# The first block of a SwiGLU feed-forward: x's parts in another order, and two of its eight pairs in groups of seven products

## The chip, the cores and the metric

The kernel runs on one core of a Trainium2 chip. The metric is the device time of one execution in microseconds. Three runs of the kernel before took 2275.22, 2275.67 and 2276.53 us; their median is 2275.67.

The engines are called as in the profile: PE (TensorE) does the matrix products, DVE (VectorE) and ACT (ScalarE) the elementwise work, SP issues nearly all the DMA transfers. Each engine takes its instructions in the order in which the program issued them.

## What is computed

The reference is one decoder layer on 256 tokens of width 2048, in float32. The change lies in the very first matrix product of it, `x @ w_gu`:

```python
def swiglu(x, w_gu, w_down):
    g, u = jnp.split(x @ w_gu, 2, axis=-1)
    return (jax.nn.silu(g) * u) @ w_down

h = layer_norm(alpha * h + 0.5 * swiglu(h, w_ffn1_gu[i], w_ffn1_down[i]), ln_g[i, 0], ln_b[i, 0])
# then: retention and attention branches, gated and mixed; layer_norm
h = layer_norm(alpha * h + 0.5 * swiglu(h, w_ffn2_gu[i], w_ffn2_down[i]), ln_g[i, 2], ln_b[i, 2])
# then: a gated embedding; layer_norm
```

`w_gu` is 2048 x 11264 and `w_down` 5632 x 2048.

## The kernel before

**Numbers in two parts.** Every operand of a product is held as a high part (a copy in the reduced type float32r, made by ACT, line 100) and a low part (value minus high part, made by DVE, line 101). A product of two values is three matrix instructions: low by high, high by high, high by low (lines 376, 377, 378, `Sum.add`). Each is 128 x 128 by 128 x 512.

**Blocks, pairs and units.** The gate and up stage of the first feed-forward ("f1") runs over 11 blocks. A block has 512 columns of the gate half and 512 of the up half, for 256 tokens (two halves of 128), so four outputs of 128 x 512, each in a bank of PSUM: `f1g` (two) and `f1u` (two). The 2048 rows of the weight are taken in eight pairs of 128-row steps, numbered 0 to 7. A plain pair (letter "P") is two units (`Single`): one 512 KB weight transfer for the gate columns, then one for the up columns, with 12 matrix instructions each.

**Seven products.** A pair with letter "S" (`Seven`) does the 2 x 2 by 2 x 2 product of its quarters in seven products in place of eight, so 21 matrix instructions for 24. It loads the same two transfers, makes four sums of quarters of the weight on DVE (lines 172 to 175), the high and low parts of seven of the quarters and sums, and needs four sums of quarters of x as well: the "forms" (`seven_forms`, lines 447 to 450, then a cast and a low part). Forms 0 serve pairs 0 and 1, forms 1 pairs 2 and 3. Four of the seven products go to sums of their own, p1, p6, p7 and q5, a PSUM bank each, shared by all S pairs of the block; the other three go to outputs. Behind the block's last S pair the `fold` (`seven_common`) copies p1 to SBUF on ACT (line 481), and combines it with p6 (482), p7 (483) and q5 (484, 485) on DVE; at the block's end the four outputs are added (line 964), and Silu and the gate product follow. A block without S pairs has neither: two Silu on ACT (line 970), two products on DVE (line 972). In f1, block 0 is "PPPPPPPP" with pairs 0 to 7 in order, odd blocks are "PPSPSPSP" (pairs 0, 1, 2 as S, and the others in order between them), even blocks "PPSSPSSP" (0 to 3 as S). In the last S pair of a block the products for the four own sums come first, p1, q5, p6, p7.

**PSUM.** The pool has eight banks. A bank is given to a tile at its first product and comes back when its last reader has been issued; it is taken in the order in which banks came back.

**x.** x comes in four parts of 128 x 4 x 256 (512 KB, `xraw`); part c serves pairs 2c and 2c + 1. `load_x_chunk` issues the transfer and the split into `xt`. Part 0 is loaded in three pieces with the first two weight units; part 1 directly behind; parts 2 and 3 at positions 2 and 4 of block 0 (`first_chunk`). The parts are kept for the forms, both of which are made at position 7 of block 0.

**The order of the work.** The program is written in one order, and a small planner puts loads and conversions into it. `fill` is called whenever a unit is `done`: it converts the next loaded unit as long as the converted ones stand for less than 45 units of time (12 for a plain unit, 21 for a grouped pair) and slots are left, and issues loads while converted and loaded ones stand for less than 90. Slots are SBUF tiles of 4 KB a partition; the planner is allowed 9 of them at first and 24 from position 6 of block 0. `block` calls `before(u)` ahead of position u: that is where x's parts, the constants (four small transfers issued by ACT, lines 806 to 809) and the forms come in. In a grouped pair, `done(u)`, and so `fill`, comes before `fold`.

```python
            for to, left, right in steps:
                to.add(left, right)
            done(u)
            run_side()
            if p == sevens[-1]:
                fold(p1.ap, p6.ap, p7.ap, q5.ap)
```

Of the kernel before, what the change touches and what calls it, by code (L numbers as in the profile page):

```python
# [38 lines left out]


SEVEN = (0, 1, 2, 3)


AHEAD = (4, 5)
# [13 lines left out]
def layer(ctx: ExitStack, tc: tile.TileContext, io):  # L58
# [13 lines left out]
    def banks(name):  # L72
        return [bank(name + str(j)) for j in range(2)]

    def slot(shape, dt, name):
        return slots.tile(shape, dt, tag="slot", name=name)
# [225 lines left out]
    def slots_for_weights(n, ahead=45, far=90):  # L302
        room.update(slots=n, ahead=ahead, far=far)
# [136 lines left out]
    def seven_forms(full, hi, lo):  # L440


        a11, a21 = (full[:, 0::2, t * P : (t + 1) * P] for t in range(2))
        a12, a22 = (full[:, 1::2, t * P : (t + 1) * P] for t in range(2))
        raw = slot([P, 8, P], F32, "sums")
        f5, f6, f7, f3 = (raw[:, 2 * j : 2 * j + 2, :] for j in range(4))
        dve.tensor_tensor(f5, a21, a22, ALU.subtract)
        dve.tensor_tensor(f7, a11, a21, ALU.subtract)
        dve.tensor_tensor(f6, f5, a11, ALU.subtract)
        dve.tensor_tensor(f3, a12, f6, ALU.add)  # L450
        split(hi, lo, raw)
        return lambda e: [(hi[:, 2 * j + e, :], lo[:, 2 * j + e, :]) for j in range(4)]
# [9 lines left out]
    def forms_of(parts, name):  # L462
        hi, lo = (slot([P, 8, P], F32R, name + w) for w in "hl")
        return seven_forms(whole(parts, name + "w"), hi, lo)

    def units_of(order, sevens, ahead=()):

        sevens, ahead = list(sevens), list(ahead)
        plain = [p for p in range(KD // 2) if p not in sevens + ahead]
        of = {"S": sevens, "D": ahead, "P": plain}  # L470
        return [(kind, of[kind].pop(0)) for kind in order]
# [6 lines left out]
    def seven_common(p1, p6, p7, q5):  # L478

        e, w = slot([P, 2, 512], F32, "eve"), slot([P, 2, 512], F32, "evw")  # L480
        act.copy(e[:, 0], p1)
        dve.tensor_tensor(w[:, 0], e[:, 0], p6, ALU.add)
        dve.tensor_tensor(e[:, 1], w[:, 0], p7, ALU.add)
        dve.tensor_tensor(w[:, 0], q5, w[:, 0], ALU.subtract)
        dve.tensor_tensor(w[:, 1], q5, e[:, 1], ALU.subtract)
        return e, w
# [6 lines left out]
    def plan_tokens(key, n_k, nk=2):  # L493
        for c in range(n_k // nk):
            plan.append(Single(key + (c,)))
# [309 lines left out]
    def load_constants():  # L805
        act.dma_start(cst, io["cst"])
        act.dma_start(mask, io["mask"])
        act.dma_start(gn, io["gn"])
        act.dma_start(sink, io["att_sinks"].broadcast_to([P, HA]))
# [42 lines left out]


    def gu_units(name, j):
        if j == 0:
            return [("P", p) for p in range(KD // 2)]
        if name == "f2" and j in AHEAD_BLOCKS:
            return units_of("PPSDSDSP", SEVEN[:3], AHEAD)
        order = "PPSSPSSP" if j % 2 == 0 else "PPSPSPSP"
        return units_of(order, SEVEN[: order.count("S")])  # L860

    def gu_keys(name, j):
        return lambda n, p: (name + "_gu", j, n, p)
# [26 lines left out]
    def ffn(name, i, ht, norm, keep, residual, keepers, away):  # L890
# [23 lines left out]
        def convert(g):  # L914
            hi, lo = (slot([P, 4, S], F32R, f"{name}a{w}{g}") for w in "hl")
            split(hi, lo, raws[g])
            acts[g] = hi, lo

        for j in range(KF // 4):
            pg, pu = banks(f"{name}g{j}"), banks(f"{name}u{j}")  # L920
            units = gu_units(name, j)
            n_of = {(0, 0): KD, (0, 1): KD, (1, 0): KD, (1, 1): KD}
            for kind, p in units:
                if kind != "P":
                    for at in ((0, 0), (0, 1), (1, 0)):
                        n_of[at] -= 1
                    n_of[1, 1] -= 2
            sums = [[Sum((pg, pu)[n][t], n_of[t, n]) for n in range(2)] for t in range(2)]
            got = []

            if norm is not None and j == 0:
                front, units = units[:FRONT_PAIRS], units[FRONT_PAIRS:]
                steps = [(gu_keys(name, 0)(n, p), 2 * p, n) for _, p in front for n in range(2)]
                norm.first(steps, rhs, sums, (
                    (3, (1, 0)), (5, "more"), (5, (1, 1)), (7, (0, 2)), (8, (1, 2)), (9, (0, 3)), (10, (1, 3)), (10, "go"),
                ))
                slots_for_weights(24)

            def before(u, j=j, offset=KD // 2 - len(units)):
                u += offset  # L940
                if j == 0 and norm is None and u % 2 == 0:
                    first_chunk(u // 2)
                    if u == 6:
                        slots_for_weights(24)
                    if u == 2:
                        load_constants()
                if j == 0 and u == 7:
                    for g in sorted({p // 2 for p in SEVEN}):
                        hi, lo = (slot([P, 8, P], F32R, f"{name}f{w}{g}") for w in "hl")
                        made[g] = seven_forms(keep[g], hi, lo)  # L950
                    if name == "f2":
                        g = AHEAD[0] // 2
                        made[g] = forms_of([ht[:, 4 * g : 4 * g + 4, :]], f"{name}f{g}")
                if name == "f2" and j in AHEAD_BLOCKS and u == 0:
                    slots_for_weights(AHEAD_SLOTS - j)
                if j == KF // 4 - 1 and u in (4, 6):
                    convert(u // 2 - 2)

            block(f"{name}{j}", units, gu_keys(name, j), rhs, forms, sums, lambda *a: got.extend(seven_common(*a)), before)
            if got:  # L960
                g, v = got
                for x, ps in ((g, pg), (v, pu)):
                    for t in range(2):
                        dve.tensor_tensor(x[:, t], x[:, t], ps[t], ALU.add)  # L964
                act.activation(g, g, AF.Silu)  # L965
                dve.tensor_tensor(v, g, v, ALU.mult)
            else:
                v = slot([P, 2, 512], F32, f"{name}v{j}")
                for t in range(2):
                    act.activation(v[:, t], pg[t], AF.Silu)  # L970
                for t in range(2):
                    dve.tensor_tensor(v[:, t], v[:, t], pu[t], ALU.mult)
            later(2, lambda j=j, v=v: turned(j, v))
# [71 lines left out]
        norm = Norm((2, 3), sums, combine, y, stats, i, 4 * LN_EPS, keepers, away, (0, 3))  # L1045
# [55 lines left out]
    def later(n, job):  # L1101
        for j in range(n):
            if len(side) <= j:
                side.append(idle)
        side.insert(n, job)
# [515 lines left out]
            held_out(steps, lhs, [[s] for s in sums], lambda t, j: None, first_done, lambda n: None, 0)  # L1621
            last_half()

    def first_chunk(c):

        if c == 0:
            load_x_chunk(0)
            fill()
        if c < 3:
            load_x_chunk(c + 1)  # L1630

    x_parts = {}

    def load_x_chunk(c):
        raw = slot([P, 4, S], F32, f"xraw{c}")
        x_parts[c] = raw
        if c:
            sync.dma_start(raw, io["xT"][c])
            split_x(c, slice(0, 4))
            return  # L1640
        parts = [slice(0, 1), slice(1, 2), slice(2, 4)]
        for at in parts:
            sync.dma_start(raw[:, at], io["xT"][c][:, at])
        for queue in (act, sync):
            u = plan.pop(0)
            u.load(pieces=2, queue=queue)
            u.chunk.make_hi()
            room["used"] += u.keeps
            ready.append(u)
        first, second = (u.chunk for u in ready)  # L1650
        split_x(c, parts[0])
        first.make_part(first.parts[0])
        split_x(c, parts[1])
        first.make_part(first.parts[1])
        for at in second.parts:
            second.make_part(at)
        split_x(c, parts[2])

    def split_x(c, at):
        to = ht[:, 4 * c : 4 * c + 4, :][:, at]  # L1660
        split(to[:, :, :S], to[:, :, S:], x_parts[c][:, at])
# [7 lines left out]
    with tc.manual_schedule():  # L1669
# [9 lines left out]
        for blk in range(4):  # L1679
            plan_tokens(("w_pg", blk), KD)  # L1680
        kept = sorted({p // 2 for p in SEVEN})
        warm_up()
        norm = ffn("f1", 0, ht, None, x_parts, x_columns, (), rows[0])
        norm = mixers(norm.new, norm, rows[0], kept, rows[1])
        norm = ffn("f2", 2, norm.new, norm, norm.keep, rows[1], (), None)
# [102 lines left out]
```

## Time and profile before

| | |
|---|---|
| median of three runs | 2275.67 us |
| the profiled execution's own time | 2275.11 us |
| its span, first to last instruction | 2273.3 us |
| PE busy | 2265.6 us (100%), 10509 products |
| PE weight loads | 1882.3 us (83%) |
| DVE busy | 1981.4 us (87%), 2562 operations |
| ACT busy | 1220.3 us (54%), 1485 operations |
| DMA, mean over the span | 222 GB/s, 505.75 MB |
| block 0's last product starts | 49.40 us |

In rows of the timeline the columns are: start in us, duration in us, engine, line, operation, output <- inputs, shapes, count, and in brackets the idle time of the engine before the row and what ended it. "xcount" rows merge several instructions, and their duration is then from the first start to the last end. The products are pipelined, so the distance from one start to the next, not the duration, is the rate. In rows by stretch of time the numbers behind the length are the busy time and count of PE, weight loads, DVE, ACT and POOL, then the granted clock of TensorE, the share of the DMA engines, and GB/s. Tile names carry no numbers: `hf_gu` and `lf_gu` are the high and low part of a weight unit of the feed-forwards, `rf_gu` the raw transfer, `uf_gu` and `vf_gu` the sums of a grouped pair with `huf_gu`, `luf_gu`, `hvf_gu`, `lvf_gu` their parts, `bf_gu` one quarter's parts, `f11s` the four sums of block 1, `eve` and `evw` the fold's results.

### The profile page before, as it was taken

What the parts mean: (1) busy time and instruction counts of PE and PEld (TensorE: products, weight loads), DVE (VectorE), ACT (ScalarE), POOL (GpSimd) and SP (SyncE); (2) the same over time, 40 slices, a digit from 0 to 9 for tenths busy, and PEclk for the clock granted to TensorE, in tenths of its full rate; (3) what the DMA queues carried; (4) which work ended last, traced back from release to release, by engine and by line L of the source; (5) the groups of instructions that cost most, each with busy time, mean ns of one, the idle gap of its engine ahead of it and who ended that gap; (6) DMA issues with size and microseconds to landing.
All of it is one profiled execution on the core that took longest, in us unless ns stands there. A gap on an engine that the chain in (4) does not pass through costs nothing.

```text
span 2273.3 us, 29101 instructions
## 1 busy us (share of the span) xinstructions
PE 2265.6 (100%) x10509; PEld 1882.3 (83%) x10509; DVE 1981.4 (87%) x2562; ACT 1220.3 (54%) x1485; POOL 2.3 (0%) x9
## 2 busy tenths in 40 slices
PE   9999999999999999999999999999999999999999
PEld 8888888888888888888778888888888888888887
DVE  7999999999889887787789787789999999889887
ACT  6555555556555444544566454555565556555543
POOL 0000000000000000000000000000000000000000
PEclk9999999999999999999999999999999999999999
DMA  8666665665587789655446567787767766555772
GB/s 301 206 202 197 197 210 179 205 203 190 207 287 260 257 306 308 222 163 170 141 157 222 186 210 269 293 287 234 266 218 253 254 198 218 194 203 197 282 272 74
DMA packets 207736, 505.75 MB, mean 222 GB/s; under 512 B 16092, under 2 KB 20060, under 8 KB 207592
## 3 DMA queue, kind: packets, MB, share of 16 engines
q1 hardware_dynamic: 205608, 501.32, 65.5%
q10 hardware_dynamic: 1984, 2.58, 0.4%
q8 instruction: 82, 1.34, 0.2%
q14 instruction: 62, 0.51, 0.1%
HBM read 478.67 MB, written 25.17 MB: 222 GB/s over the span
## 4 chain that ended last, share of the span: by engine, by line
PE 95%; DVE 2%; DMA 1%; issue 1%; ACT 0%; ACTq 0%; POOL 0%; SPq 0%; DVEq 0%; POOLq 0%
PE f1g L377 3%; PE f1g L376 3%; PE f1g L378 3%; PE f2g L378 3%; PE f2g L376 3%; PE f2g L377 3%; PE rqk L327 3%; PE f1u L377 2%; PE f1u L376 2%; PE f1u L378 2%; PE f2u L376 2%; PE f2u L378 2%; PE f2u L377 2%; PE aqk L327 2%; PE f1d L378 2%; PE f1d L376 2%
## 5 line engine op out<-in xcount | busy, mean ns | idle before, releaser
L101 DVE TENSOR_TENSOR lf_gu<-rf_gu,hf_gu 128x1024 fp32r<-128x1024 f32 (+1 forms) x276 | 325.6, 1212 | 13.5 <-ACT hf_gu L100 12.7
L100 ACT CAST hf_gu<-rf_gu 128x1024 fp32r<-128x1024 f32 (+1 forms) x276 | 275.8, 1044 | 29.5 <-DMA rf_gu<-in_f_gu 23.8
L101 DVE TENSOR_TENSOR lf_down<-rf_down,hf_down 128x1024 fp32r<-128x1024 f32 x152 | 181.2, 1220 | 23.7 <-ACT hf_down L100 19.0
L101 DVE TENSOR_TENSOR lw_in_f<-rw_in_f,hw_in_f 128x1024 fp32r<-128x1024 f32 x140 | 167.4, 1219 | 34.5 <-ACT hw_in_f L100 34.0
L100 ACT CAST hf_down<-rf_down 128x1024 fp32r<-128x1024 f32 x152 | 155.4, 1051 | 77.0 <-DMA rf_down<-in_f_down 20.5
L100 ACT CAST huf_gu<-uf_gu 128x1024 fp32r<-128x1024 f32 x70 | 73.8, 1055 | 146.3 <-DVE uf_gu L173 143.4
L100 ACT CAST hw_in_f<-rw_in_f 128x1024 fp32r<-128x1024 f32 x140 | 139.9, 1051 | 2.2 <-DMA rw_in_f<-in_w_in_f 1.3
L376 PE MATMUL f1g<-hf_gu,xt 128*128 128x512 f32 x247 | 96.5, 391 | 0.0
L377 PE MATMUL f1g<-hf_gu,xt 128*128 128x512 f32 x247 | 96.3, 390 | 0.0
L378 PE MATMUL f1g<-lf_gu,xt 128*128 128x512 f32 x247 | 96.3, 390 | 0.0
L100 ACT CAST hvf_gu<-vf_gu 128x1024 fp32r<-128x1024 f32 x70 | 73.9, 1055 | 29.3 <-DVE vf_gu L175 28.4
L965 ACT ACTIVATE eve<-eve 128x1024 f32<-128x1024 f32 x20 | 21.2, 1061 | 125.1 <-DVE eve L964 125.1
L376 PE MATMUL f2g<-hf_gu,ht 128*128 128x512 f32 x223 | 87.0, 390 | 0.0
L378 PE MATMUL f2g<-lf_gu,ht 128*128 128x512 f32 x223 | 86.9, 390 | 0.0
L377 PE MATMUL f2g<-hf_gu,ht 128*128 128x512 f32 x223 | 86.8, 389 | 0.0
L101 DVE TENSOR_TENSOR luf_gu<-uf_gu,huf_gu 128x1024 fp32r<-128x1024 f32 x70 | 85.3, 1219 | 0.0
L101 DVE TENSOR_TENSOR lvf_gu<-vf_gu,hvf_gu 128x1024 fp32r<-128x1024 f32 x70 | 85.3, 1219 | 0.0
L376 PE MATMUL f1u<-hf_gu,xt 128*128 128x512 f32 x212 | 83.3, 393 | 0.0
L377 PE MATMUL f1u<-hf_gu,xt 128*128 128x512 f32 x212 | 82.5, 389 | 0.0
L378 PE MATMUL f1u<-lf_gu,xt 128*128 128x512 f32 x212 | 82.5, 389 | 0.0
L376 PE MATMUL f2u<-hf_gu,ht 128*128 128x512 f32 x180 | 71.3, 396 | 0.0
L378 PE MATMUL f2u<-lf_gu,ht 128*128 128x512 f32 x180 | 70.1, 389 | 0.0
(1441 smaller groups left out, 6519.2 us busy)
## 6 DMA issues: line engine op xcount, KB each, us to landing
rf_gu<-in_f_gu SPq DMA_DIRECT2D x358, 512.0 KB
rf_down<-in_f_down SPq DMA_DIRECT2D x176, 512.0 KB
rw_in_f<-in_w_in_f SPq DMA_DIRECT2D x148, 512.0 KB
rw_rv<-in_w_rv SPq DMA_DIRECT2D x32, 512.0 KB
rw_ret<-in_w_ret SPq DMA_DIRECT2D x32, 512.0 KB
rw_mix<-in_w_mix SPq DMA_DIRECT2D x32, 512.0 KB
rw_pg<-in_w_pg SPq DMA_DIRECT2D x32, 512.0 KB
rw_att<-in_w_att SPq DMA_DIRECT2D x16, 512.0 KB
```

The costliest lines, as they stand in the source:

```text
L100: act.copy(dst_hi, src)
L101: (lo_engine or dve).tensor_tensor(dst_lo, src, dst_hi, ALU.subtract)
L327: pe.matmul(ps[f], hi[:, kk, f * P : (f + 1) * P], rhs(k), start=k == 0, stop=k == n_k - 1,)
L376: pe.matmul(o, al, bh, start=first, stop=False)
L377: pe.matmul(o, ah, bh, start=False, stop=False)
L378: pe.matmul(o, ah, bl, start=False, stop=self.left == 0)
L965: act.activation(g, g, AF.Silu)
```

## The change

Block 0 of the first feed-forward becomes "PPPPPSPS" with pairs 2 and 3 as S: its order is 0, 1, 4, 5, 6 plain, 2 grouped, 7 plain, 3 grouped. x's parts are loaded in the order 0, 2, 3, 1: part 2 directly behind part 0, part 3 at position 2, part 1 at position 3. Forms 1 are made at position 4 and forms 0 at position 7; in the second feed-forward ("f2") both stay at position 7. The planner has 24 slots from position 4. The constants are issued at position 5 in place of 2.

```diff
+X_AT = {0: 2, 2: 3, 3: 1}
...
     def gu_units(name, j):
+        if j == 0 and name == "f1":
+            return units_of("PPPPPSPS", (2, 3))
         if j == 0:
             return [("P", p) for p in range(KD // 2)]
...
-                if j == 0 and norm is None and u % 2 == 0:
-                    first_chunk(u // 2)
-                    if u == 6:
-                        slots_for_weights(24)
-                    if u == 2:
+                if j == 0 and norm is None:
+                    load_x(u)
+                    if u == 5:
                         load_constants()
-                if j == 0 and u == 7:
-                    for g in sorted({p // 2 for p in SEVEN}):
+                if j == 0 and u in (4, 7):
+                    groups = {("f1", 4): (1,), ("f1", 7): (0,), ("f2", 7): (0, 1)}
+                    for g in groups.get((name, u), ()):
                         hi, lo = (slot([P, 8, P], F32R, f"{name}f{w}{g}") for w in "hl")
                         made[g] = seven_forms(keep[g], hi, lo)
-                    if name == "f2":
+                    if (name, u) == ("f1", 4):
+                        slots_for_weights(24)
+                    if (name, u) == ("f2", 7):
                         g = AHEAD[0] // 2
                         made[g] = forms_of([ht[:, 4 * g : 4 * g + 4, :]], f"{name}f{g}")
...
-    def first_chunk(c):
-
-        if c == 0:
+    def load_x(u):
+
+        if u == 0:
             load_x_chunk(0)
             fill()
-        if c < 3:
-            load_x_chunk(c + 1)
+        if u in X_AT:
+            load_x_chunk(X_AT[u])
```

## The prediction

> **What bounds the kernel now.** First the page, engines and granted clock, then the clock view:
>
> ```profile
> PE 2265.6 (100%) x10509; PEld 1882.3 (83%) x10509; DVE 1981.4 (87%) x2562; ACT 1220.3 (54%) x1485; POOL 2.3 (0%) x9
> ```
> ```profile
> core 0: 2273.3 us, clock 0.999
> ```
>
> TensorE (PE) is never without work, so any microsecond taken off or put onto its stream early reaches the end. Then the timeline of TensorE at the first feed-forward's opening: its first products, the second weight unit (8.81), the last product of block 0, the first of block 1, and the first of block 2.
>
> ```profile
> 1.44 4.32 PE L1667 MATMUL warm<-ident 128*128 128x128 f32 x19 [1.44 <-POOL ident masks.py:199]
> 5.42 0.80 PE L376 MATMUL f1g<-hf_gu,xt 128*128 128x512 f32 x1
> 6.01 0.63 PE L377 MATMUL f1g<-hf_gu,xt 128*128 128x512 f32 x1
> 6.44 0.46 PE L378 MATMUL f1g<-lf_gu,xt 128*128 128x512 f32 x1
> 6.73 0.40 PE L376 MATMUL f1g<-hf_gu,xt 128*128 128x512 f32 x1
> 8.81 0.39 PE L376 MATMUL f1u<-hf_gu,xt 128*128 128x512 f32 x1
> 49.40 0.39 PE L378 MATMUL f1u<-lf_gu,xt 128*128 128x512 f32 x1
> 49.62 0.39 PE L376 MATMUL f1g<-hf_gu,xt 128*128 128x512 f32 x1
> 92.01 0.39 PE L376 MATMUL f1g<-hf_gu,xt 128*128 128x512 f32 x1
> ```
>
> From 8.81 to 49.62 lie 15 units of 12 products: 180 in 40.81 us, 0.2267 us each, with no gap. Block 0 runs at the rate of TensorE although its data are only just arriving. Third, how they arrive: the scalar engine's (ACT's) casts start when a transfer lands.
>
> ```profile
> 14.67 1.06 ACT L100 CAST hf_gu<-rf_gu 128x1024 fp32r<-128x1024 f32 x1 [0.30 <-DMA rf_gu<-in_f_gu]
> 16.03 1.05 ACT L100 CAST hf_gu<-rf_gu 128x1024 fp32r<-128x1024 f32 x1 [0.30 <-DMA rf_gu<-in_f_gu]
> 17.38 1.06 ACT L100 CAST hf_gu<-rf_gu 128x1024 fp32r<-128x1024 f32 x1 [0.30 <-DMA rf_gu<-in_f_gu]
> 18.66 1.05 ACT L100 CAST xt<-xraw 128x1024 fp32r<-128x1024 f32 x1 [0.22 <-DMA xraw<-in_xT]
> ...
> 19.75 1.23 DVE L101 TENSOR_TENSOR xt<-xraw,xt 128x1024 fp32r<-128x1024 f32 x1
> ```
>
> and, from the waits of SP's queue and the busy time by microsecond (last two columns: share of the DMA engines, GB/s):
>
> ```profile
> SPq L114 <- DMA cst<-in_cst: 4.3, 1, 4.3
> 25.00:26.00 1.00, 1.00 (x6) 0.84 (x5) 0.67 (x1) 0.30 (x1) 0.00 (x0) 1.00 0.51 100
> ```
>
> One 512 KB transfer lands every 1.35 us (16.03 to 17.38) and VectorE (DVE) finishes each 2.3 us after its landing (18.66 to 19.75 + 1.23). Near 25 us the stream thins to 100 GB/s, because SP stood 4.3 us behind the constants.
>
> **The change, part by part.** *Products.* Pairs 2 and 3 take 21 products each for 24: six fewer, 6 x 0.2267 = **-1.36 us** of TensorE. Expected starts from 8.81 in steps of 12 products (2.72 us): pair 2 (the tenth unit after the first) at 33.30, pair 7 at 38.06, pair 3 at 43.50, end of block 0 at 48.26.
>
> *Transfers.* Block 0 loads the same bytes. x's part 2 is issued where part 1 was, part 3 where part 2 was (position 2), part 1 at position 3, one ahead of where part 3 was; the constants move from position 2 to 5. SP thus has no constants ahead of the rest, and the thin stretch at 25 us goes. Continuing at 1.35 us after 18.66: pair 6 lands at 20.0 and 21.4, x's part 1 at 22.7, pair 2 at 24.1 and 25.4, pair 7 at 26.8 and 28.1, pair 3 at 29.5 and 30.8. That costs nothing; if it slips, see the fourth case. The constants are four issues on ACT, some 1.9 us, while ACT has a good third of its time free; their first readers come after the whole gate and up stage. Allowing 24 slots at position 4 instead of 6 issues loads earlier and makes nothing later.
>
> *VectorE.* A grouped pair makes four sums and four low parts; the forms of x (those of part 1, "forms 1", move up to position 4, ahead of pair 6; forms 0 stay at position 7) are four sums, a cast on ACT and a low part. Their rows, and those of a fold:
>
> ```profile
> 40.37 0.42 DVE L447 TENSOR_TENSOR sums<-xraw 128x256 f32<-128x256 f32 x1
> 41.49 0.43 DVE L450 TENSOR_TENSOR sums<-xraw,sums 128x256 f32<-128x256 f32 x1
> 43.10 1.23 DVE L101 TENSOR_TENSOR f1fl<-sums,f1fh 128x1024 fp32r<-128x1024 f32 x1 [1.17 <-ACT f1fh L100]
> 44.24 0.42 DVE L447 TENSOR_TENSOR sums<-xraw 128x256 f32<-128x256 f32 x1
> 51.57 0.69 DVE L172 TENSOR_TENSOR uf_gu<-rf_gu,rf_gu 128x512 f32<-128x512 f32 x1
> 54.23 1.22 DVE L101 TENSOR_TENSOR lf_gu<-rf_gu,hf_gu 128x1024 fp32r<-128x1024 f32 x1
> 57.10 1.22 DVE L101 TENSOR_TENSOR lvf_gu<-vf_gu,hvf_gu 128x1024 fp32r<-128x1024 f32 x1
> 58.24 1.22 DVE L101 TENSOR_TENSOR lf_gu<-rf_gu,hf_gu 128x1024 fp32r<-128x1024 f32 x1
> 84.12 0.69 DVE L482 TENSOR_TENSOR evw<-eve,f11s 128x512 f32<-128x512 f32 x1 [2.27 <-PE f11s L378]
> 84.91 0.69 DVE L483 TENSOR_TENSOR eve<-evw,f11s 128x512 f32<-128x512 f32 x1
> ```
>
> Forms hold VectorE 3.87 us (40.37 to 44.24), a grouped pair 6.67 (51.57 to 58.24), a plain low part 1.14 (57.10 to 58.24). VectorE works in program order, and by the planner's counts that order is: low parts up to x's part 1; forms 1; pair 2; pair 7 (two); pair 3; block 1's first pair, 3 (two); forms 0; block 1's second pair, 4 (two, because `done` fills before `fold` is called); then the fold. Part 1 lands at 22.7, its low part starts 1.09 us later (18.66 to 19.75) and the next operation 1.14 after that: 24.95. From there: forms 1 to 28.8, pair 2 to 35.5, pair 7 to 37.8, pair 3 to 44.4, two low parts to 46.7, forms 0 to 50.6, two low parts to **52.85**: 3.87 + 6.67 + 2.28 + 6.67 + 2.28 + 3.87 + 2.28 = 27.9 us.
>
> Operands within block 0 are just in time, cost nothing: pair 2's first low part is ready at 28.8 + 2.66 (51.57 to 54.23) + 1.22 = 32.7, its third product needs it at 33.75; the last low part is ready at 35.6, wanted at 37.1; pair 3 follows the same way, its last low part at 44.5 for 45.3.
>
> *The end of the block.* Block 0 now ends in a grouped pair, and its PSUM banks are all taken: four outputs and four group sums are the pool's eight. Block 1's four outputs must take the group sums' banks: the first when ACT has copied sum p1 (L481), the second when VectorE has read p6 (L482), then p7, then q5. In later blocks a plain pair lies between: the fold at 84.12 is 7.9 us ahead of block 2's first product at 92.01, so nothing waits there. Here the first copy stands on ACT behind forms 0's cast and two weight casts: forms 0's sums start at 46.7 and end 1.55 later (40.37 to 41.49 + 0.43), three casts at 1.05 and the copy at 0.6 bring 52.0 us. L482 ends at 52.85 + 0.69 = 53.55. TensorE, done at 48.26, waits 3.7 us, runs three products (0.68 us), and waits again, to 53.6: its fourth product comes at 53.6 and not at 48.94, **+4.66 us**. p7 is read by 55.1 (two steps of 0.79 after 52.85, as 84.12 to 84.91, and their 0.69) and wanted at 55.6: no third wait. The other fold operations, four additions and a product then put block 1's first group at about 59.3 to 66 on VectorE; its first low part is ready near 63.1 and wanted at 65 at the earliest. At block 1's first product the planner holds what it held before (36 units of time ready, 45 loaded), so later blocks are issued in the same order. A kept gain or a further loss there I put at nothing.
>
> *The clock.* No row shows TensorE pausing 4 us. The nearest are the two ends of the kernel:
>
> ```profile
> 2267.09 0.96 PE L1561 MATMUL pln<-lnrow,plnst 66*128 66x512 f32 x3 [0.21 <-DVE plnst L1559]
> 2269.00:2270.00 1.00, 0.00 (x0) 0.00 (x0) 0.00 (x0) 0.00 (x0) 0.00 (x0) 0.79 0.94 342
> 2270.00:2271.00 1.00, 0.00 (x0) 0.00 (x0) 0.00 (x0) 0.00 (x0) 0.00 (x0) 0.50 1.00 375
> ```
>
> The products end at 2268.05, and the granted clock falls to half by about 2269.6, 1.5 us later. So a pause of 3.7 us probably halves it. Starting from low, the products came 0.43 us apart (6.01 to 6.44) and reached full pace near 6.73, 5.3 us after the first work at 1.44. A pause therefore costs between nothing (no fall) and 5.3 x (1 - 0.2267 / 0.43) = 2.5 us. Counting the 5.3 us from the restart at 52.0, of which 53.6 to 57.3 delays the stream, gives 3.7 x 0.47 = **+1.7 us**, which I take, as it follows the row of the start.
>
> Sum against the profiled execution (2275.11 us for a span of 2273.3): -1.36 + 4.66 + 1.7 = +5.0, 2280.1; against the median of the runs, 2275.67 (0.56 above that execution), **2280.7 us**.
>
> **The rivals.**
> *The clock stays up.* Then the sum is +3.3: **2279.0 us**. For it: the fall at the end was seen with nothing following, and 0.68 us of work splits the pause. Against it: 1.5 us was enough there. [...]
>
> *No wait at the block's end.* If the copy and L482 came before the forms and the low parts in the engines' order, or VectorE stood 4.7 us less deep in its queue, the banks would be free at 48.3 and only the products would count: 2275.67 - 1.36 = **2274.3 us**, within the measurement. It decides when L482 starts before 48.3 instead of 52.85. For it: VectorE is idle often before 40 us now. Against: the 27.9 us above start only at x's part 1, at 24.95, and none of them can be passed over in an in-order queue.
>
> *The transfers do not keep their pace.* If they land as slowly as around 25 to 33 us now:
>
> ```profile
> 32.00:33.00 1.00, 1.00 (x6) 0.84 (x5) 0.11 (x1) 0.86 (x1) 0.00 (x0) 1.00 0.82 260
> ```
>
> 512 KB at 260 GB/s is 2.0 us, 0.67 more; three of them put x's part 1, and the whole queue, 2.0 us later. Pair 2 would wait about 1 us of it and the end the rest: 2280.7 + 2.0 = **2282.7 us**. For it: eight large transfers were under way there too. Against: that stretch had the constants' small packets in it.
>
> **How the numbers follow.** Wait and slow clock 0.55 (own range 2279.8 to 2282, the clock at 0.8 to 2.5 us and VectorE's queue to half a microsecond); wait, full clock 0.20; no wait 0.10; slow transfers 0.15. The range 2278.0 to 2283.6 leaves out the case without a wait and the far end of the last. A change under 0.2% (4.55 us, beyond 2280.2) can hardly be told from none: of the first case about 0.38 lies above, of the last all: slower 0.54. Same: 0.17 + 0.20 + 0.08 = 0.45. Faster: 0.01, there being only 1.36 us to win.
>
> **What would show it.** Matrix products: six fewer. VectorE: six more operations per grouped pair, four in the fold, three in the eviction, 19 in all. The timeline: x's part 1 cast near 22.7, L447 first near 25, L482 of block 0 near 52.9, and TensorE's idle time before block 1's first two outputs put down to ACT L481 and DVE L482, some 3.7 and 1 us. The granted clock by microsecond: half somewhere between 51 and 58. The prediction fails if TensorE waits inside pairs 2 or 3 (operands late), if L482 starts before 48.3, or if a second wait opens in block 1.

## The result and the profile after

The changed kernel takes 2280.92 us, the median of 15 runs (2279.92 to 2282.3); the kernel before, run beside it 15 times, 2275.22 us (2274.4 to 2277.23). The ratio is 1.0025 with a 95% interval of 1.0018 to 1.0032: slower by 5.7 us. The profiled execution took 2280.09 us, 4.98 more than that of before (2275.11). It is the second shortest of the 15: what its profile shows accounts for about 5 us of the 5.7. Its mean granted clock is 0.999; nine of the others, all of them longer, show 0.998, which suggests that their clock was low for longer, but no profile shows it.

From the page, the engines and the core's span and granted clock:

```profile
PE 2265.9 (99%) x10503; PEld 1881.6 (83%) x10503; DVE 1994.1 (88%) x2581; ACT 1222.5 (54%) x1489; POOL 2.3 (0%) x9
```
```profile
core 0: 2278.0 us, clock 0.999
```

Six products fewer, 19 VectorE operations and four ACT operations more. TensorE's busy time is unchanged to 0.3 us (2265.9 for 2265.6), though six products worth 1.36 us are gone: some of the others took longer. The rest is idle time. Where it lies, from the timeline of TensorE after the change (start, duration, operation, and in brackets the idle time and its releaser), from block 0's last product on:

```profile
48.61 0.39 PE L380 MATMUL f1g<-lvf_gu,xt 128*128 128x512 f32 x1
53.01 0.73 PE L378 MATMUL f1g<-hf_gu,xt 128*128 128x512 f32 x1 [4.00 <-ACT eve L483]
53.53 0.63 PE L379 MATMUL f1g<-hf_gu,xt 128*128 128x512 f32 x1
53.96 0.63 PE L380 MATMUL f1g<-lf_gu,xt 128*128 128x512 f32 x1
54.76 0.80 PE L378 MATMUL f1g<-hf_gu,xt 128*128 128x512 f32 x1 [0.17 <-DVE evw L484]
55.35 0.63 PE L379 MATMUL f1g<-hf_gu,xt 128*128 128x512 f32 x1
56.59 0.39 PE L379 MATMUL f1g<-hf_gu,xt 128*128 128x512 f32 x1
```

Block 0 ends with its grouped pair 3. Block 1's first output takes the bank of p1, which comes free when ACT has copied it (L483, line 481 of before); the first product waits 4.0 us for it. Three products later the second output needs the bank of p6, free when VectorE has added it (L484, before 482). The products between are 0.43 us apart (53.53 to 53.96) instead of 0.23, because the clock fell meanwhile. By microsecond (after the length: busy time and count of PE, weight loads, DVE, ACT, POOL, then the granted clock, DMA share, GB/s):

```profile
52.00:53.00 1.00, 0.00 (x0) 0.00 (x0) 1.00 (x2) 0.95 (x2) 0.00 (x0) 1.00 0.00 0
53.00:54.00 1.00, 0.99 (x3) 0.77 (x3) 1.00 (x1) 0.00 (x0) 0.00 (x0) 0.55 0.00 0
54.00:55.00 1.00, 0.83 (x3) 0.24 (x2) 0.90 (x3) 0.00 (x0) 0.00 (x0) 0.50 0.00 0
55.00:56.00 1.00, 1.00 (x3) 0.81 (x4) 0.97 (x2) 0.00 (x0) 0.00 (x0) 0.50 0.50 111
56.00:57.00 1.00, 1.00 (x4) 0.81 (x4) 1.00 (x3) 0.00 (x0) 0.00 (x0) 0.74 0.87 279
```

A mean of 0.55 is half speed for 0.9 us, so the clock was low from 53.1 to 56.5. Why the two banks were late, from the timelines of ACT and VectorE after the change:

```profile
23.97 1.05 ACT L102 CAST xt<-xraw 128x1024 fp32r<-128x1024 f32 x1 [1.05 <-DMA xraw<-in_xT]
49.53 1.04 ACT L102 CAST f1fh<-sums 128x1024 fp32r<-128x1024 f32 x1 [4.82 <-DVE sums L452]
50.48 1.99 ACT L102 CAST hf_gu<-rf_gu 128x1024 fp32r<-128x1024 f32 x2
52.38 0.57 ACT L483 COPY eve<-f10s 128x512 f32<-128x512 f32 x1
```
```profile
26.19 0.42 DVE L449 TENSOR_TENSOR sums<-xraw 128x256 f32<-128x256 f32 x1
...
45.60 2.35 DVE L103 TENSOR_TENSOR lf_gu<-rf_gu,hf_gu 128x1024 fp32r<-128x1024 f32 x2
47.87 0.42 DVE L449 TENSOR_TENSOR sums<-xraw 128x256 f32<-128x256 f32 x1
...
51.75 2.35 DVE L103 TENSOR_TENSOR lf_gu<-rf_gu,hf_gu 128x1024 fp32r<-128x1024 f32 x2
54.02 0.68 DVE L484 TENSOR_TENSOR evw<-eve,f10s 128x512 f32<-128x512 f32 x1
```

The copy had to wait for forms 0's cast, which waited 4.8 us for VectorE's sums (47.87 and on), and for two weight casts. The fold stands behind block 1's low parts, forms 0 and more low parts, 27.8 us after the first sum of forms 1 (26.19 to 54.02). VectorE had no idle time in between but the 1.2 us in each set of forms in which it waits for ACT's cast.

The same product can be compared in both profiles. The opening of the kernel took 0.54 us longer (the thirteenth product starts at 9.35, before at 8.81). Six products save 1.36, so block 0's last product starts 0.79 us sooner (48.61 for 49.40). The waits then add 4.5 and the slow products 1.7: from there to 2170 us every product is 5.4 to 5.5 us late. About 0.8 come back behind 2171 us. That last shift is in the profiles of all the experiments too, 0.3 to 0.8 us, so it most likely belongs to the one profiled execution of before.

### The profile page after: what moved, and what is told of

Same layout as the page of the kernel before. It is cut to its first block, busy times and chain, and to the rows that moved or that the text cites. A ratio compares the mean times of both kernels' runs of the same rounds, so it can differ in the third digit from the quotient of the medians.

```text
span 2278.0 us, 29121 instructions
## 1 busy us (share of the span) xinstructions
PE 2265.9 (99%) x10503; PEld 1881.6 (83%) x10503; DVE 1994.1 (88%) x2581; ACT 1222.5 (54%) x1489; POOL 2.3 (0%) x9
## 4 chain that ended last, share of the span: by engine, by line
PE 98%; DVE 1%; DMA 1%; issue 0%; ACT 0%; ACTq 0%; DVEq 0%
PE f1g L378 3%; PE f1g L380 3%; PE f1g L379 3%; PE f2g L380 3%; PE f2g L378 3%; PE f2g L379 3%; PE rqk L329 3%; PE f1u L380 2%; PE f1u L379 2%; PE f1u L378 2%; PE f2u L378 2%; PE f2u L380 2%; PE f2u L379 2%; PE aqk L329 2%; PE f1d L379 2%; PE f1d L378 2%
## 5 line engine op out<-in xcount | busy, mean ns | idle before, releaser
L378 PE MATMUL f1u<-hf_gu,xt 128*128 128x512 f32 x204 | 80.3, 393 | 0.0
L379 PE MATMUL f1u<-hf_gu,xt 128*128 128x512 f32 x204 | 79.4, 389 | 0.0
```

The costliest lines, as they stand in the source:

```text
L378: pe.matmul(o, al, bh, start=first, stop=False)
L379: pe.matmul(o, ah, bh, start=False, stop=False)
```

## The experiments

The first theory: the fold stands too late in VectorE's queue, so the banks are late, TensorE waits, and its clock falls. If its place is all that is at fault, issuing it sooner gives the 1.36 us. A rival: the new order of x and the constants costs something by itself. The first four runs led to a wider theory, the "backlog" of the later expectations: VectorE's queue is too long by the work of two groupings, and TensorE pays wherever it first needs something from it. All edits are made in the changed kernel, and each is compared with runs of the kernel before on the same chip: 2275.2 us for the first four below, 2274.78 for the next four, 2274.89 for the last two.

**The order alone.** All eight pairs plain, x, constants, forms 1 and slots as in the change.

```diff
-            return units_of("PPPPPSPS", (2, 3))
+            return [("P", p) for p in (0, 1, 4, 5, 6, 2, 7, 3)]
```

> x's parts, forms, slots and constants as in the changed kernel, the pairs of block 0 in the same order 0 1 4 5 6 2 7 3, but all plain. No fold, no group sums, so block 1's outputs find free banks, and no product is saved. Theory: as before the change, 2275.2 us within 0.5. Rival, that the order of x's parts or the later constants cost something by themselves: above 2276.

Measured: 2275.06 us (2274.28 to 2276.08) beside 2275.2 of before, ratio 1.0000 (0.9991 to 1.0009), no wait of TensorE from 3 to 300 us. The order costs nothing that can be seen here, and the loss belongs to the groups.

**The fold ahead of the next conversions.**

```diff
             for to, left, right in steps:
                 to.add(left, right)
+            if p == sevens[-1] and name == "f10":
+                fold(p1.ap, p6.ap, p7.ap, q5.ap)
             done(u)
             run_side()
-            if p == sevens[-1]:
+            if p == sevens[-1] and name != "f10":
                 fold(p1.ap, p6.ap, p7.ap, q5.ap)
```

> Block 0's fold is issued ahead of the filling behind its last grouped pair, so ahead of two weight casts on ACT (1.99 us there) and two low parts on VectorE (2.28 us). Theory of the queue: L484 of block 0 starts 2.28 us sooner than the 54.0 us of the changed kernel, the copy L483 some 1.9 us sooner; the first wait shrinks from 4.2 to about 2.3 us. [...] Rival, that block 1's products wait for their own weights or for something else than the banks: no change, 2280.9, or more, as the weights' low parts now come later.

Measured: 2277.99 us (2277.26 to 2279.27), ratio 1.0012 (1.0004 to 1.0021). TensorE's waits (the copy and the reading of p6 are lines 485 and 486 here), and the clock by microsecond:

```profile
PE f1g L378 <- ACT eve L485: 2.1, 1, 2.1
PE f1g L378 <- DVE evw L486: 0.4, 1, 0.4
```
```profile
51.00:52.00 1.00, 0.75 (x3) 0.48 (x3) 1.00 (x2) 1.00 (x2) 0.00 (x0) 1.00 0.09 33
52.00:53.00 1.00, 0.60 (x2) 0.38 (x2) 0.90 (x2) 1.00 (x2) 0.00 (x0) 0.54 0.02 8
53.00:54.00 1.00, 1.00 (x3) 0.78 (x3) 0.97 (x2) 0.09 (x1) 0.00 (x0) 0.50 0.08 16
54.00:55.00 1.00, 1.00 (x4) 0.74 (x3) 1.00 (x3) 0.00 (x0) 0.00 (x0) 0.50 0.00 0
55.00:56.00 1.00, 1.00 (x5) 0.81 (x4) 1.00 (x2) 0.00 (x0) 0.00 (x0) 0.75 0.00 0
```

The two low parts and two casts passed over take two of the four microseconds away, 2.9 us of the time. Forms 0 still stand ahead of the fold. The first wait, counted from the last product's end (48.74 + 0.23) to 51.25, is 2.3 us, as the theory of the queue said, and the rival's 2280.9 did not come. The clock halved all the same, to 0.50: it falls after a pause of only 2.1 us, at 52.1, when TensorE has been at work again since 51.25.

**Forms 0 later.** Forms 0 made at position 0 of block 1 in place of position 7 of block 0; the fold where the change has it.

```diff
-                    groups = {("f1", 4): (1,), ("f1", 7): (0,), ("f2", 7): (0, 1)}
+                    groups = {("f1", 4): (1,), ("f2", 7): (0, 1)}
...
+                if name == "f1" and j == 1 and u == 0:
+                    hi, lo = (slot([P, 8, P], F32R, f"{name}f{w}0") for w in "hl")
+                    made[0] = seven_forms(keep[0], hi, lo)
```

> Forms 0 are made at position 0 of block 1, behind block 0's fold and additions, in place of position 7 of block 0. Theory of the queue: L484 starts 3.87 us sooner, near 50.2 us, and the copy on ACT no longer stands behind the forms' cast, so TensorE has no first wait and one of some 1.3 us ahead of its fourth product of block 1; no slow clock after so short a pause. Time: 2280.9 - 6.2 (both waits and the slow products of the changed kernel) + 1.3 = 2276.0 us. Rival, that the banks come free by TensorE's own course and not VectorE's: 2280.9. Rival, that a pause of 1.3 us already halves the clock: 2277 to 2277.7.

Measured: 2277.61 us (2277.21 to 2278.24), ratio 1.0011 (1.0002 to 1.002). The waits:

```profile
PE f11s L380 <- DVE lf_gu L103: 1.6, 1, 1.6
PE f1g L378 <- DVE evw L484: 1.2, 1, 1.2
```

At the block's end 1.2 us are left, as the theory said, and the clock stays up at both waits: the granted clock is 1.00 from 48 to 56 us and from 60 to 68. The 2276.0 expected were missed by 1.6 us, because a new wait opens in block 1: its first grouped pair (pair 0) gets its low part late, since forms 0 now stand ahead of it. The time is that of the rival in which a pause of 1.3 us halves the clock (2277 to 2277.7), but by chance: the clock did not fall.

**Both edits.**

> Both edits: fold ahead of the filling, and forms 0 behind it. VectorE reaches the fold near 47.9 us, before block 0 ends, so no wait at the block's end and no slow clock; what is left is six products fewer. Theory: 2275.2 - 1.4 = 2273.9 us. Rival, that the grouped pairs cost TensorE something inside block 0 (operands just in time) or that forms 0 then make block 1's first grouped pair late: 2275.2 or more.

Measured: 2278.91 us (2277.28 to 2280.55), ratio 1.0017 (1.0008 to 1.0026). The 2273.9 that the first theory gave was missed by 5 us. The waits at the block's end are gone, as it said; what came is the rival's late first grouped pair of block 1. VectorE and TensorE in block 1:

```profile
56.85 0.42 DVE L451 TENSOR_TENSOR sums<-xraw 128x256 f32<-128x256 f32 x1
60.66 0.68 DVE L174 TENSOR_TENSOR uf_gu<-rf_gu,rf_gu 128x512 f32<-128x512 f32 x1
63.31 1.22 DVE L103 TENSOR_TENSOR lf_gu<-rf_gu,hf_gu 128x1024 fp32r<-128x1024 f32 x1
```
```profile
64.58 0.79 PE L380 MATMUL f11s<-lf_gu,xt 128*128 128x512 f32 x1 [3.04 <-DVE lf_gu L103]
```

The first low part of pair 0 is ready at 64.5 (63.31 + 1.22), and TensorE, not held back before, wants it 3 us sooner; the clock falls there instead, at 0.76, 0.50, 0.50 and 0.53 by microsecond from 64 to 68 us. In the changed kernel the same low part starts at 63.11, as early, and costs nothing only because TensorE has just lost six microseconds. So the first theory falls: it is not the fold's place alone, but a debt of VectorE's, which is paid at whatever point TensorE first needs something from it.

**Pair 3 before pair 7**, so that a plain pair lies between fold and block's end.

```diff
-            return units_of("PPPPPSPS", (2, 3))
+            return units_of("PPPPPSSP", (2, 3))
```

> Block 0 as PPPPPSSP: pair 3 is grouped right behind pair 2, and plain pair 7 is last, so the fold has 5.4 us of products behind it. If only the place of the fold mattered, the time would be 2275.2 - 1.4 = 2273.9 us. If VectorE's backlog is what is paid for, the wait moves into pair 3: its low parts follow pair 2's 6.67 us of VectorE work while TensorE needs 4.76, so it waits some 3 us in two or three pieces inside pair 3 and none at the block's end: 2277.6 us.

Measured: 2278.2 us (2277.26 to 2279.27), ratio 1.0014 (1.0005 to 1.0023), where the backlog gave 2277.6 and the place of the fold alone 2273.9. The waits are now inside pair 3, none at the block's end, and the clock stays up in the profiled execution, which took 2277.26 us at a mean granted clock of 1.0:

```profile
PE f10s L380 <- DVE lf_gu L103: 1.1, 1, 1.1
PE f10s L380 <- DVE luf_gu L103: 0.8, 1, 0.8
```

**Two extra VectorE operations ahead of the fold** (128 x 1024, of x's first part with itself; nobody reads the result), the suspected cause made larger by 2 x 1.14 us.

```diff
+                if name == "f10":
+                    longer()
                 fold(p1.ap, p6.ap, p7.ap, q5.ap)
...
+    def longer():
+        w = slot([P, 4, S], F32, "longer")
+        for _ in range(2):
+            dve.tensor_tensor(w, x_parts[0], x_parts[0], ALU.add)
```

> The changed kernel with two more VectorE operations of 128x1024 (1.14 us each) ahead of block 0's fold, whose results nobody reads. Theory of the queue: L484 starts 2.28 us later, and the second wait at the block's end grows by the same, while the copy on ACT and so the first wait stay as they are; the pause is then split in two. Time 2280.9 + 2.3 = 2283.2 us, and up to 1 us more if the clock stays low through the longer second wait. Rival, that the end of the block is bound by ACT's copy alone: 2280.9.

Measured: 2284.24 us (2283.17 to 2285.33), ratio 1.004 (1.0028 to 1.0053), 3.3 us above the changed kernel, or 3.8 when each is taken over its own runs of before (9.5 for 5.7). The waits, and the clock:

```profile
PE f1g L378 <- ACT eve L485: 4.0, 1, 4.0
PE f1g L378 <- DVE evw L486: 2.5, 1, 2.5
```
```profile
52.00:53.00 1.00, 0.20 (x1) 0.20 (x2) 1.00 (x2) 0.75 (x2) 0.00 (x0) 0.65 0.00 0
53.00:62.00 9.00, 6.50 (x15) 4.62 (x16) 8.72 (x12) 1.76 (x2) 0.00 (x0) 0.50 0.22 62
62.00:63.00 1.00, 1.00 (x5) 0.81 (x4) 1.00 (x2) 0.75 (x2) 0.00 (x0) 0.73 0.78 168
```

ACT's wait is unchanged and VectorE's grows by 2.3 us, the length of the two operations: the reading of p6 (L486 here) is what the second output waits for. The rest, 1 to 1.5 us, goes with the clock, which now stays low from 52.3 to 62.5: product by product, the profile loses 1.8 us more in slow products than that of the changed kernel.

**Forms 0 by GpSimd** (POOL), with the fold first: the four sums at position 2 and the low part at position 6 of block 0, so VectorE is rid of 3.87 us, less the wait for the cast.

```diff
...
+                if name == "f1" and j == 0 and u == 2:
+                    hi, lo = (slot([P, 8, P], F32R, f"{name}f{w}0") for w in "hl")
+                    made[0], made["rest"] = forms_by_pool(keep[0], hi, lo)
+                if name == "f1" and j == 0 and u == 6:
+                    made["rest"]()
...
+        pool.tensor_tensor(f5, a21, a22, ALU.subtract)
+        pool.tensor_tensor(f7, a11, a21, ALU.subtract)
+        pool.tensor_tensor(f6, f5, a11, ALU.subtract)
+        pool.tensor_tensor(f3, a12, f6, ALU.add)
```

> Fold ahead of the filling, and forms 0 made by GpSimd: its four sums at position 2, the cast on ACT and the low part on GpSimd at position 6. VectorE has 3.87 us less to do before block 1's first grouped pair. Theory of the backlog: fold near 48 us, no wait at the block's end, first low part of block 1's pair 0 near 60.7 us, before TensorE wants it (61.1): no wait at all, 2273.9 us. Rival, that GpSimd and VectorE slow each other: VectorE's 128x1024 low parts take longer than 1.14 us from start to start while GpSimd works, and some of the 3.87 us comes back: up to 2277.

Measured: 2278.01 us (2275.19 to 2278.68), ratio 1.0011 (1.0002 to 1.002). Both expected times, 2273.9 and at most 2277, were missed: the median is no better than with VectorE. The executions fall in two groups, five of 2275.19 to 2276.94 and six of 2278.01 to 2278.68, with a mean granted clock of 0.999 to 1.0 in the first and 0.998 to 0.999 in the second. The profile is one of the first group (2276.72), and its mean granted clock is 1.0, so no fall is seen; what the second group lost is not shown. The wait at the block's end is gone there, but one of 2.1 us is now inside pair 3. GpSimd and VectorE at that place, and in the opening:

```profile
9.85 1.07 POOL L467 TENSOR_TENSOR sums<-xraw,sums 128x256 f32<-128x256 f32 x1
44.30 2.92 POOL L103 TENSOR_TENSOR f1fl<-sums,f1fh 128x1024 fp32r<-128x1024 f32 x1 [33.37 <-PE f1u L379]
```
```profile
10.25 1.23 DVE L103 TENSOR_TENSOR xt<-xraw,xt 128x512 fp32r<-128x512 f32 x1
44.90 3.41 DVE L103 TENSOR_TENSOR lvf_gu<-vf_gu,hvf_gu 128x1024 fp32r<-128x1024 f32 x1
```

VectorE's low part, 1.22 us elsewhere, takes 3.41 and ends at 48.31, 1.09 after GpSimd has ended at 47.22: it seems to have done its work only then. The low part in the opening takes 1.23 us for 0.69 in the changed kernel. Some 2 of the 2.7 us of work taken off VectorE are lost to the neighbour at the one place, and TensorE waits there.

**One group.** Pair 2 alone grouped, in the same place.

```diff
-            return units_of("PPPPPSPS", (2, 3))
+            return [("S" if p == 2 else "P", p) for p in (0, 1, 4, 5, 6, 2, 7, 3)]
```

> The same order of pairs, but pair 2 alone is grouped: three products fewer, 0.68 us. VectorE has 4.4 us less to do than in the changed kernel, the fold has two plain units' pair 7 and pair 3 behind it. Theory of the backlog: no wait at the block's end and at most a few tenths at block 1's first grouped pair: 2275.2 - 0.7 = 2274.5 us. Rival, that any fold in block 0 makes block 1 wait: 2276 or more.

Measured: 2275.97 us (2275.22 to 2276.45) beside 2274.78, ratio 1.0005 (0.9996 to 1.0013). The block's end is free, as the theory said, but the 2274.5 expected were missed by 1.5 us: pair 2 itself waits a little. The rival's number (2276 or more) comes near, but its wait, in block 1, did not come.

```profile
PE f10s L380 <- DVE luf_gu L103: 0.8, 1, 0.8
PE f10s L380 <- DVE lvf_gu L103: 0.2, 1, 0.2
```

Its operands come behind forms 1, and so behind x's part 1, which is cast at 24.12 and so lands too late for this place. The next two runs show that a later place is enough; whether an earlier part 1 alone would be was not tested.

**One group, one pair later**, behind pair 7; and the same with x's part 1 one transfer earlier (`X_AT = {0: 2, 2: 1, 3: 3}`).

```diff
-            return units_of("PPPPPSPS", (2, 3))
+            return [("S" if p == 2 else "P", p) for p in (0, 1, 4, 5, 6, 7, 2, 3)]
```

> Pair 2 alone in seven products, as in the run with one group, but behind pair 7: the order is 0, 1, 4, 5, 6, 7 plain, 2 grouped, 3 plain. Everything else (x's order, forms 1 at position 4) as in the changed kernel. If VectorE was merely a little late for pair 2 in the run with one group (its own operands, 1.8 us of waits), 5.4 us more of room makes them vanish, and the fold lies a whole plain pair ahead of the block's end: no wait anywhere in blocks 0 and 1, three products fewer, 0.68 us off the kernel before, about 2274.5. If instead every grouping in block 0 leaves a debt that TensorE pays, the waits come back in another place (pair 2, pair 3, or block 1's first grouped pair) and the time is 2275.2 or more.

> As the run before it in this call, and x's parts in the order 0, 2, 1, 3: part 1, from which forms 1 are made, is loaded at position 2 and part 3 at position 3, so VectorE can make forms 1 one transfer earlier. If VectorE has room enough already, this changes nothing: 2274.5, as that run. If pair 2 is still late there, its waits shrink by about 1.3 us. A loss could only come from part 3, now one transfer later: its low part is wanted at position 4 (27.9 us) and would be ready near 26; if it slips, a wait of TensorE at pair 6 shows it.

Measured: 2274.46 us (2273.84 to 2274.91) and 2274.13 us (2273.58 to 2274.95), beside 2274.89; ratios 0.9997 (0.9989 to 1.0006) and 0.9996 (0.9987 to 1.0005). TensorE waits nowhere in blocks 0 and 1. VectorE in the first of them:

```profile
38.44 1.22 DVE L103 TENSOR_TENSOR lvf_gu<-vf_gu,hvf_gu 128x1024 fp32r<-128x1024 f32 x1
39.57 4.63 DVE L103 TENSOR_TENSOR lf_gu<-rf_gu,hf_gu 128x1024 fp32r<-128x1024 f32 x4
44.11 0.68 DVE L484 TENSOR_TENSOR evw<-eve,f10s 128x512 f32<-128x512 f32 x1
```

The last low part of pair 2 is ready at 39.7, with the pair's products from 39.1 to 43.8, and the fold begins at 44.11, some 5 us ahead of block 1 (49.28). One grouping fits into VectorE's idle time of block 0; two did not, in either of the places tried. The sizes fit: from 20 to 50 us VectorE stood idle for 8.5 us in the kernel before, and its busy time over the whole kernel grows by 8.0 us with one group (1989.4 for 1981.4) and by 12.7 with two (1994.1). The gain expected, 0.68 us, agrees with the medians' 0.43 and 0.76, but both intervals hold 1: these are the only versions with groups in block 0 whose profiles show no wait, and whether they win can't be told at this spread.

## Why the prediction was right

The time (2280.92 for 2280.7) and its mechanism came as forecast. That the two times agree to 0.2 us is partly luck: the loss forecast was 5.0 us, over a median of 2275.67 for before, and the loss measured is 5.7, over 2275.22. Point by point:

- *Six products, -1.36 us*: six fewer, and the block's last product is over at 48.84 (48.61 + 0.23). Forecast was 48.26; 0.54 of the 0.58 is the later opening, where TensorE waited 0.6 us for an early weight cast.
- *Transfers at 1.35 us, x's part 1 at 22.7*: mis-sized. It landed at 23.97, 1.3 us late: ACT's casts up to there are spaced 1.3 to 1.5 us, and ACT then stood 1.05 us idle for this one transfer. In size that is two thirds of the 2.0 us of the rival with slow transfers, but not by its mechanism: the thin stretch went, and the stream moved 367 to 410 GB/s in every microsecond from 18 to 26, where the rival had 260. Why this one transfer came late stays open; the cast of the last of x's parts starts between 23.6 and 24.4 us in every experiment as well.
- *VectorE's chain, 27.9 us*: 27.8 us from L449 to L484 (26.19 to 54.02), operation by operation in the order worked out; all of the delay at its end, 1.17 us, was there at its start (26.19 for 24.95).
- *First wait 3.7, second about 1.0*: 4.2 us from the last product's end to 53.01, then only 0.4, as ACT's copy was late by 1.0 us (52.95 for 52.0) and VectorE's by 1.15 (54.70 for 53.55), and the three products between ran at half speed. The sum of waits, 4.5, is near the 4.66, for partly other reasons: the late transfer added about one microsecond, the later end of block 0 took half of it away, and the slow products hid most of the second wait.
- *The clock, +1.7 us*: 1.7 us. The term has the right size, but by luck and not by the right times: it was counted from the restart for 5.3 us, to 57.3, and the clock was low from 53.1 to 56.5, 3.4 us, of which nearly all was worked in.
- *Operands within pairs 2 and 3 just in time*: no wait in the changed kernel's profile. But the margin was thinner than thought: with pair 2 in the same place, the runs with the fold first and with forms 0 later show a wait of 0.2 us in it, and the run with one group lost 1.8 us there, counted product by product. With pair 3 directly behind pair 2 the waits in pair 3 were 1.1 and 0.8 us.
- *No further loss in block 1*: held in the changed kernel, and the working did give it room (a low part ready at 63.1, wanted at 65 or later; it was ready at 64.3 and wanted at 67.3). The runs show on what it rested: when TensorE isn't held back at the block's end, the same low part is 3 us late.
- *The rival without a wait* was priced as one condition (L482 before 48.3). The runs show that it isn't enough: with the fold at 48.16 the loss moved to block 1. A time like its 2274.3 came only when a whole grouping was taken out and the other put later, and that with three products saved and not six.
- *The rival with the clock up* fell: it was half for 3.4 us. That does not make the fall after 1.5 us at the trace's end a rule: with forms 0 later, pauses of 1.2 and 1.6 us left the clock up, at 1.00.

## What to carry to other kernels

Count the queue of the helping engine over the whole stretch, from the last moment it was idle to the next, and not only to the first wait: if its added work exceeds its idle time there, expect the other engine to wait, and moving the operation that is waited for may just move the wait. Saving 0.23 us of TensorE a product is worth nothing where each such saving puts more work on a second engine than that has room for; here 4.4 us a pair, and a fold and its additions besides, for 0.68. And where a block ends in work that needs its banks back, price a pause of TensorE with the clock it may lose, here about 1.7 us on top.

## What was not expected of the hardware

In the four profiles in which the clock fell at the end of block 0 or in block 1, its low stretches were whole multiples of one length: 0.9 + 2 + 0.52 = 3.42 us in the changed kernel, 0.92 + 2 + 0.5 = 3.42 with the fold first, 0.48 + 2 + 0.94 = 3.42 with both edits (the two whole microseconds in the middle stand at 0.50 in all three), and 10.2 = 3 x 3.41 with the two extra operations (half speed from 52.3 to 62.54, by means of 0.65 and 0.73 in the outer microseconds). The fall came at different places behind a pause: with the fold first at 52.1, when TensorE had been busy for 1.28 of the 3.4 us before, in the changed kernel at 53.1, when it had been for 0.10. Of two pauses of 2.1 us, the one with the fold first halved the clock and the one in the run with GpSimd did not (mean granted clock 1.0); one of 1.6 us (forms 0 later) left it up as well. So pauses of 2.1, 3.0 and 4.0 us cost a whole low stretch in these runs, and another of 2.1 none. What decides it is not shown: no run moves a pause alone.

In the one run that tried it, a low part of VectorE took 3.41 us beside one of GpSimd, for 1.22 elsewhere (above), so GpSimd was no free helper for a busy VectorE there.

The opening differs by up to 0.94 us between profiled executions (the thirteenth product at 8.53 us with GpSimd and at 9.47 in the last run), more than a single group can win. The shift at 2171 us in the profile of before stays unexplained.
